# The retention's values from seven products of quarter matrices, with sums of weights on VectorE and by adding DMAs

## Chip, cores and metric

One core of a Trainium2 chip runs the whole program in one launch. The metric is the device time of one execution in microseconds (us). Differences are against the kernel before; its runs lie within 0.13 us of one another.

## What is computed

The input x is [512, 1024] (512 tokens). It is rms-normed and multiplied with w_in into ten parts of 1024 columns; two branches use them and are merged by gates.

```python
h = rms_norm(x, norm_gain)
proj = einsum('bsd,dc->bsc', h, w_in)
(sb_q, sb_k, sb_v, sb_g, r_q, r_k, r_v, r_g, m_sb, m_ret) = split(proj)
out_a = merge_heads(stick_breaking_attention(norm(sb_q), norm(sb_k), sb_v)) * silu(sb_g)   # 8 heads
ret   = chunkwise_retention(rotary(r_q), rotary(r_k) * 256**-0.5, r_v)                     # 4 heads
out_b = merge_heads(rms_norm(ret, ret_out_gain)) * silu(r_g)
merged = sigmoid(m_sb + b0) * (out_a @ w_branch_sb) + sigmoid(m_ret + b1) * (out_b @ w_branch_ret)
x = x + merged @ w_out
```

The change touches r_v, the values of the retention: a product of [512, 1024] by [1024, 1024].

## The kernel before

Every fp32 number is split into a high part that TensorE takes without loss and a low part, the rest; a product is three matmuls (high·high, high·low, low·high).

The program is a row of **groups**, each of 512 output columns: `dense` (called by `proj`) goes through 8 blocks of 128 rows of the weights (k), and for each adds three matmuls 128x512 into each of 4 PSUM banks: 96 matmuls. `load_split` fetches the weights in four pieces of 512 KB (raw, two buffers), and splits each: a cast on ScalarE writes hi, a subtraction on VectorE writes lo (`split`), each with two buffers. A piece serves two k, that is 24 matmuls. The groups before stand in this order: qk0, v0, sg0, qk1, qk2, v1, sg1, qk3, rv0, ma0, pa0, ma1, pa1, rqk0, rg0, rqk1, rv1, rqk2, rg1, rqk3, mb0, mb1, pb0, pb1, fin0, fin1. Here v is the attention's values, sg its gate, ma and mb the merge gates, pa, pb and fin the products with the three last weights; rqk0 to rqk3 are q and k of one retention head each, rg its gate, rv its values (two heads in each group).

**Side work.** Attention and retention are generators in the `Interleaver`. A group calls `work.step()` after every second bank, 15 times in a group; the generator then gives out its next matmuls if its counter has run down (`W_RQ` = 8 steps ahead of the first scores of a retention head, `W_RZ` = 2 between them). So the order on TensorE is that of the code; matmuls and the loads on SyncE's queue keep it. ScalarE, VectorE and GpSimd take their instructions in an order that the scheduler sets when the program is built, and each of them works through its list in that order.

**Rope.** `rope_group` takes the four banks of rqk: 12 products and sums on VectorE (rm), two copies on ScalarE (rk), and four splits into rqk_hi, rqk_lo (quarters q0, q1, k0, k1). `retention` then multiplies these into scores rz (rz0_0 is the first of head 0: six matmuls 128x512), decays them into wT (pf), and multiplies by rv.

GpSimd has small work: the normalisation of the attention's q and k (qraw), and of the retention's output (roraw). All DMAs are issued by SyncE or ScalarE.

Of the kernel before, what the change touches and what calls it, by code (L numbers as in the profile page):

```python
# [66 lines left out]
@with_exitstack  # L67
def hybrid_block(ctx, tc, x, x_t, vecs, w_in, w_a, w_b, w_o, cos_t, sin_t, decay, out):
    nc = tc.nc
# [96 lines left out]

    idle = const.tile([P, S], mybir.dt.bfloat16, name="idle")
# [174 lines left out]

# [108 lines left out]

    def retention(h, qk, v, gates):
        hi, lo = qk
        dec = tmp.tile([P, S], F32, tag="dec", bufs=1, name=f"dec{h}")
        load(dec, decay[h])
        pT = wT_pair
        yield W_RQ
        for i in range(NT):
# [191 lines left out]
```

## Time and profile before

| | |
|---|---|
| time, median of 3 runs | 664.40 us (664.32 to 664.45) |
| time of the profiled execution | 664.18 us |
| its span in the trace | 662.4 us, so 1.8 us lie around it |
| granted clock of TensorE, mean over the span | 1.0 of full |
| busy: TensorE, VectorE, ScalarE, GpSimd | 99%, 57%, 39%, 8% |
| bytes by DMA | 65.02 MB, mean 98 GB/s |

Busy is the share of the span in which an engine had an instruction running. A group below is a line of the kernel, an engine, an operation and its tiles; a timeline gives the start and the duration of each instruction. The durations of matmuls are modelled and overlap, so the pace of TensorE is read from starts.

### The profile page before, as it was taken

How to read it: one execution, taken by the hardware profiler on the slowest of the kernel's cores; microseconds unless marked ns; L12 is line 12 of the kernel's file. 1: busy time of each engine (PE TensorE's matmuls, PEld its weight loads, DVE VectorE, ACT ScalarE, POOL GpSimd, SP SyncE). 2: the span in 40 equal slices, each digit the busy share in tenths (PEclk: the TensorE clock that was granted, in tenths of full speed). 3: DMA queues.
4: the chain of work that ended last, by engine and by line, in shares of the span. 5: the costliest groups of instructions: out<-in, count | busy, mean ns of one | idle time of the engine just before them, and what ended most of it. 6: DMA issues, size and time to landing. Idle time of an engine off the chain costs nothing.

```text
span 662.4 us, 7979 instructions
## 1 busy us (share of the span) xinstructions
PE 656.3 (99%) x3096; PEld 546.4 (82%) x3096; DVE 375.9 (57%) x560; ACT 260.7 (39%) x416; POOL 50.8 (8%) x50
## 2 busy tenths in 40 slices
PE   8999999999999999999999999999999999999997
PEld 5888888888888888888888888888888888888886
DVE  6456874587497477632334763844862953544632
ACT  4744534464364554422312342433433443422310
POOL 0051000441000400000000001001001001000000
PEclk9999999999999999999999999999999999999999
DMA  8543223322322323233333323222323322335541
GB/s 288 189 128 96 65 63 96 96 64 65 95 64 64 96 63 96 60 99 96 95 96 111 96 64 106 84 80 81 96 70 106 93 66 64 96 95 161 158 159 63
DMA packets 42182, 65.02 MB, mean 98 GB/s; under 512 B 2848, under 2 KB 19488, under 8 KB 42144
## 3 DMA queue, kind: packets, MB, share of 16 engines
q1 hardware_dynamic: 41568, 63.47, 31.2%
q10 hardware_dynamic: 576, 1.05, 0.4%
q8 instruction: 24, 0.39, 0.3%
q14 instruction: 14, 0.11, 0.1%
HBM read 62.41 MB, written 2.10 MB: 97 GB/s over the span
## 4 chain that ended last, share of the span: by engine, by line
PE 99%; DMA 0%; SPq 0%; ACT 0%; DVE 0%; issue 0%; DVEq 0%; ACTq 0%
PE qk_ps L86 14%; PE rqk_ps L86 13%; PE sg_ps L86 7%; PE v_ps L86 7%; PE ma_ps L86 7%; PE rv_ps L86 7%; PE mb_ps L86 7%; PE rg_ps L86 7%; PE fin_ps L86 7%; PE pb_ps L86 7%; PE pa_ps L86 7%; PE po L86 2%; PE z L86 2%; PE rz L86 2%; PE ro L86 2%; PE pw L89 1%
## 5 line engine op out<-in xcount | busy, mean ns | idle before, releaser
L86 PE MATMUL qk_ps<-qk_hi,xT_hi 128*128 128x512 f32 x128 | 51.5, 411 | 0.9 <-ACT xT_hi L159 0.9
L86 PE MATMUL rqk_ps<-xT_hi,rqk_hi 128*128 128x512 f32 x128 | 50.5, 394 | 0.0
L86 PE MATMUL rqk_ps<-xT_hi,rqk_lo 128*128 128x512 f32 x128 | 50.0, 391 | 0.0
L86 PE MATMUL rqk_ps<-xT_lo,rqk_hi 128*128 128x512 f32 x128 | 50.0, 390 | 0.0
L86 PE MATMUL qk_ps<-qk_lo,xT_hi 128*128 128x512 f32 x128 | 49.8, 398 | 0.0
L86 PE MATMUL qk_ps<-qk_hi,xT_lo 128*128 128x512 f32 x128 | 49.5, 395 | 0.0
L86 PE MATMUL pb_ps<-ob,pb_hi 128*128 128x512 f32 x128 | 39.5, 390 | 0.0
L86 PE MATMUL pa_ps<-oa,pa_hi 128*128 128x512 f32 x128 | 39.4, 389 | 0.0
L116 DVE TENSOR_TENSOR rqk_lo<-rqk_raw,rqk_hi 128x1024 fp32r<-128x1024 f32 x16 | 20.8, 1300 | 23.9 <-ACT rqk_hi L115 23.9
L386 DVE TENSOR_TENSOR_SCAN keep<-keep,zero 128x128 f32<-128x128 f32 (+3 forms) x32 | 27.1, 847 | 7.3 <-ACT keep L384 7.3
L86 PEld LDWEIGHTS qk_ps<-qk_hi,xT_hi 128*128 128x128 f32 x128 | 24.5, 192 | 6.2 <-ACT xT_hi L159 1.8
L86 PEld LDWEIGHTS qk_ps<-qk_hi,xT_lo 128*128 128x128 f32 x128 | 24.5, 191 | 5.4
L189 POOL TENSOR_TENSOR rrr<-ms,m_half 128x4 f32<-128x4 f32 x4 | 4.0, 1007 | 316.3 <-DVE ms L188 316.3
L86 PEld LDWEIGHTS qk_ps<-qk_lo,xT_hi 128*128 128x128 f32 x128 | 24.7, 193 | 4.3
L86 PEld LDWEIGHTS rqk_ps<-xT_hi,rqk_lo 128*128 128x128 f32 x128 | 24.1, 188 | 5.0
L86 PEld LDWEIGHTS pb_ps<-ob,pb_hi 128*128 128x128 f32 x128 | 24.0, 188 | 5.0
L86 PEld LDWEIGHTS pa_ps<-oa,pa_hi 128*128 128x128 f32 x128 | 24.0, 188 | 5.0
L86 PEld LDWEIGHTS rqk_ps<-xT_hi,rqk_hi 128*128 128x128 f32 x128 | 24.1, 188 | 4.7
L86 PEld LDWEIGHTS rqk_ps<-xT_lo,rqk_hi 128*128 128x128 f32 x128 | 24.1, 188 | 4.6
L115 ACT CAST rqk_hi<-rqk_raw 128x1024 fp32r<-128x1024 f32 x16 | 16.8, 1050 | 25.8 <-PE rqk_ps L86 16.5
L116 DVE TENSOR_TENSOR qk_lo<-qk_raw,qk_hi 128x1024 fp32r<-128x1024 f32 x14 | 17.6, 1259 | 15.1 <-ACT qk_hi L115 15.1
L86 PE MATMUL v_ps<-v_hi,xT_hi 128*128 128x512 f32 x64 | 26.1, 408 | 0.0
(185 smaller groups left out, 1709.8 us busy)
## 6 DMA issues: line engine op xcount, KB each, us to landing
rqk_raw<-in_w_in SPq DMA_DIRECT2D x32, 256.0 KB, 3.0
qk_raw<-in_w_in SPq DMA_DIRECT2D x28, 256.0 KB, 3.0
v_raw<-in_w_in SPq DMA_DIRECT2D x8, 512.0 KB, 3.9
sg_raw<-in_w_in SPq DMA_DIRECT2D x8, 512.0 KB, 3.6
rv_raw<-in_w_in SPq DMA_DIRECT2D x8, 512.0 KB, 3.6
ma_raw<-in_w_in SPq DMA_DIRECT2D x8, 512.0 KB, 3.6
pa_raw<-in_w_a SPq DMA_DIRECT2D x8, 512.0 KB, 3.9
rg_raw<-in_w_in SPq DMA_DIRECT2D x8, 512.0 KB, 3.6
```

The costliest lines, as they stand in the source:

```text
L86: tc.keep_in_program_order(nc.tensor.matmul(*a, **k))
L89: tc.keep_in_program_order(nc.tensor.transpose(*a))
L115: nc.scalar.copy(hi, src)
L116: nc.vector.tensor_sub(lo, src, f32(hi))
L189: nc.gpsimd.tensor_tensor(dst, t[:, :width], m_half[:, :width], op=ALU.pow)
L386: nc.vector.tensor_tensor_scan(keep[:, :n][:, ::-1], keep[:, :n][:, ::-1], zero.broadcast_to([P, n]), 1.0, op0=ALU.mult, op1=ALU.add,)
```

## The change

The groups rv0 and rv1 go. The stack of weights of r_v is taken in quarters B11, B12, B21, B22 of 512x512 (a new input, laid out in quarters), and the tokens in quarters x11 to x22 of 512 (k) by 256 (tokens). Seven products of [256 x 512] by [512 x 512] replace the eight that the quarters would take (Strassen's scheme, in Winograd's form), each of 24 matmuls 128x512 into two banks: 168 in place of 192. They stand in a row between rg0 and rqk1, with no side work between their matmuls, in the order x11, x12, s1, n4, s2, s3, x22. The order of groups becomes ..., qk3, ma0, rqk0, pa0, ma1, pa1, rg0, seven products, rqk1, rqk2, rg1, rqk3, mb0, ...

- **Sums of tokens** (`token_sums`, at the start of rg0): x is loaded once more in two loads of 1 MB (xs0, xs1), ScalarE scales it in 8 instructions, GpSimd makes four sums of 128x1024, and each is split (s1, s3, s2, n4).
- **Sums of weights** (`quarter_sums`): of the four, two are made by VectorE behind the split of the tile (four adds 128x1024), and two by DMAs that GpSimd issues and that add into their destination (four of 512 KB). There are 14 pieces to split in place of 8, each used by 12 matmuls in place of 24. Pieces 1, 4, 7, 10 and 13 have their own buffers (bk, three), the others the groups' two.
- **Sums of products** (`put` in `v_groups`): products x11, s2, s3 and x22 add up in one pair of banks (y); in between VectorE takes y away from c3 and from c5.
- The retention's first scores start when `work.steps` has grown by 8 since the group of the head ended; before, the generator was first resumed at the first step and waited 8 more, which made 9.
- Buffers: beta and keep share a tag (bk), sq, rc and idle use tmp, rk uses qraw, the tiles O and V become fewer and larger.

```diff
+    def add_from(dst, src):
+        nc.gpsimd.dma_start(dst, src, accum_op=ALU.add)
...
+    def made_sums(name, t):
+        hi, lo = (O_tile(f"{name}_{q}").rearrange("p a (b t) -> p (a b) t", b=2) for q in ("hi", "lo"))
+        split(hi, lo, t)
+        sums[name] = (hi, lo)
+    def token_sums():
+        xt = [V_tile(f"xs{hf}", F32) for hf in range(2)]
+        for hf in range(2):
+            load(xt[hf], x_t[4 * hf * P : 4 * (hf + 1) * P, :].rearrange("(k p) t -> p k t", p=P))
+        yield 4
+        for hf in range(2):
+            for k in range(4):
+                r = xt[hf][:, k, :]
+                nc.scalar.activation(r, r, AF.Copy, scale=vec[:, V_NG + 4 * hf + k : V_NG + 4 * hf + k + 1])
+        (x11, x21), (x12, x22) = halves(xt[0]), halves(xt[1])
+        nc.gpsimd.tensor_sub(x22, x21, x22)
+        nc.gpsimd.tensor_sub(x21, x11, x21)
+        yield 5
+        made_sums("s1", x22)
+        nc.gpsimd.tensor_sub(x22, x22, x11)
+        yield 2
+        made_sums("s3", x21)
+        yield 2
+        nc.gpsimd.tensor_add(x12, x12, x22)
+        made_sums("s2", x22)
+        yield 2
+        made_sums("n4", x12)
...
+    def quarter_sums(name, w, room):
+        n = [0]
+        def pair():
+            n[0] += 1
+            if n[0] % 3 == 1:
+                return bk_tile(f"{name}_bhi{n[0]}", F32R), bk_tile(f"{name}_blo{n[0]}", F32R)
+            return [
+                wpool.tile([P, 2, S], F32R, tag=f"w{q}", name=f"{name}_{q}{n[0]}") for q in ("hi", "lo")
+            ]
+        def part(t, h):
+            return t[:, 2 * h : 2 * h + 2, :]
+        def made(src):
+            hi, lo = pair()
+            split(hi, lo, src)
+            return hi, lo
+        X, Y, W, Z = room
+        with tc.high_priority():
+            for h in range(2):
+                load(part(X, h), part(quarter(w, B11), h))
+                load(part(Y, h), part(quarter(w, B12), h))
+            load(W, quarter(w, B21))
+            load(Z, quarter(w, B22))
+        for h in range(2):
+            with tc.high_priority():
+                got = made(part(X, h))
+                nc.vector.tensor_add(part(X, h), part(X, h), part(Y, h))
+                add_from(part(Y, h), part(quarter(w, B22), h))
+            yield got
+        for h in range(2):
+            with tc.high_priority():
+                got = made(part(W, h))
+            yield got
+        for h in range(2):
+            with tc.high_priority():
+                got = made(part(X, h))
+                nc.vector.tensor_add(part(X, h), part(X, h), part(Z, h))
+                add_from(part(W, h), part(X, h))
+            yield got
+        for t in (Z, X, Y, W):
+            for h in range(2):
+                with tc.high_priority():
+                    got = made(part(t, h))
+                yield got
+    def product(ps, left, pieces, first):
+        for h in range(2):
+            hi, lo = next(pieces)
+            for j in range(2):
+                js = slice(j * P, (j + 1) * P)
+                for i in range(2):
+                    k = 2 * h + i
+                    a, b = (t[:, k, js] for t in left), (hi[:, i, :], lo[:, i, :])
+                    ahi, alo = a
+                    for n, (u, v) in enumerate(((ahi, b[0]), (ahi, b[1]), (alo, b[0]))):
+                        matmul(
+                            ps[j], u, v, start=first and k == n == 0, stop=k == 3 and n == 2,
+                            skip_group_check=True,
+                        )
+                work.step()
+    def strassen(name, w, room, put):
+        def banks(n):
+            return [ps_mm.tile([P, S], F32, tag="mm", name=f"{name}_{n}{j}") for j in range(2)]
+        pieces = quarter_sums(name, w, room)
+        y = banks("y")
+        for n, a in ((1, "x11"), (2, "x12"), (5, "s1"), (3, "n4"), (6, "s2"), (7, "s3"), (4, "x22")):
+            ps = y if n in (1, 6, 7, 4) else banks(f"p{n}")
+            product(ps, tokens(a), pieces, n in (1, 2, 3, 5))
+            put(n, ps)
...
+    def v_groups(name, w):
+        hi, lo = [V_tile(f"{name}0_hi")], [V_tile(f"{name}0_lo")]
+        kept = {}
+        def put(n, ps):
+            for j in range(2):
+                with tc.high_priority():
+                    if n in (1, 5, 3):
+                        c = tmp.tile([P, S], F32, tag="qraw", bufs=4, name=f"{name}_c{n}{j}")
+                        if n == 3:
+                            nc.vector.tensor_add(c, ps[j], kept[5, j])
+                        else:
+                            nc.scalar.copy(c, ps[j])
+                        kept[n, j] = c
+                    elif n == 2:
+                        c = kept[1, j]
+                        nc.vector.tensor_add(c, ps[j], c)
+                    elif n in (6, 7):
+                        c = kept[3 if n == 6 else 5, j]
+                        nc.vector.tensor_sub(c, c, ps[j])
+            for j in range(2):
+                if n == 4:
+                    v_rows(hi[0], lo[0], 2 + j, ps[j])
+                elif n == 2:
+                    v_rows(hi[0], lo[0], j, kept[1, j])
+        room = [t(f"{name}_w{n}", F32) for n, t in enumerate((T_tile, V_tile, V_tile, T_tile))]
+        strassen(name, w, room, put)
+        hi.append(V_tile(f"{name}1_hi"))
+        lo.append(V_tile(f"{name}1_lo"))
+        for n in (3, 5):
+            for j in range(2):
+                v_rows(hi[1], lo[1], 2 * (n == 5) + j, kept[n, j])
+        return [[(hi[g][:, sb, :], lo[g][:, sb, :]) for sb in range(NT)] for g in range(2)]
...
-    def gate_group(name, c0, vb):
+    def gate_group(name, c0, vb, ready=lambda: True):
         ps = proj(name, ((c0, S),), False)
+        work.drain(ready)
...
-    def rope_group(h):
+    def rope_group(h, ready):
 
         banks = proj(f"rqk{h}", ((C_RQ + 256 * h, 256), (C_RK + 256 * h, 256)), False)
+        work.drain(ready)
...
-    def retention(h, qk, v, gates):
+    def retention(h, qk, v, gates, made):
         hi, lo = qk
-        dec = tmp.tile([P, S], F32, tag="dec", bufs=1, name=f"dec{h}")
+        dec = bk_tile(f"dec{h}")[:, 0, :]
         load(dec, decay[h])
         pT = wT_pair
-        yield W_RQ
+        yield 2
+        while work.steps < made + W_RQ:
+            yield 1
         for i in range(NT):
             n = S - i * P
             z = side_psum(f"rz{h}_{i}")
...
     sg[1] = silu_group("sg1", C_G + S)
     qk_group(3)
     work.add(attention((6, 7), lambda: 1 in sg, lambda: v[1], lambda: sg[1]))
-    rv[0] = v_group("rv0", C_RV)
+    def ret(h, ready=lambda: True):
+        rq = rope_group(h, ready)
+        work.add(retention(h, rq, lambda: rv[h // 2], lambda: rg[h // 2], work.steps))
 
     pa = []
     for g in range(2):
         m = gate_group(f"ma{g}", C_MA + S * g, V_BM + 4 * g)
+        if g == 0:
+            ret(0, lambda: 5 in oa)
         ps = dense(f"pa{g}", branch_act(oa), w_a, ((S * g, S),), False)
         t = T_tile(f"pa{g}", F32)
         for j in range(4):
             nc.vector.tensor_mul(t[:, j, :], ps[j], m[j])
         pa.append(t)
 
-    def ret(h):
-        rq = rope_group(h)
-        work.add(retention(h, rq, lambda: rv[h // 2], lambda: rg[h // 2]))
-    ret(0)
+    work.side.insert(0, token_sums())
+    work.wait = 0
     rg[0] = silu_group("rg0", C_RG)
+    work.drain(lambda: "n4" in sums)
+    rv[0], rv[1] = v_groups("rv", w_rv)
     ret(1)
-    rv[1] = v_group("rv1", C_RV + S)
     ret(2)
     rg[1] = silu_group("rg1", C_RG + S)
     ret(3)
```

In the rows below, brackets name the semaphores that an instruction waits for: those of engines (PE, DVE, Activation, Pool) and of DMAs (DMAHW of the engines' queues, DMASW of GpSimd's); the number in a name tells buffers apart. VectorE in the group that follows rqk0, around the last splits of the rope. Before, that group is rg0:

```order
L116 TENSOR_TENSOR rg0_lo4_3130<-rg0_raw4_3127,rg0_hi4_3129 128x1024 [waits DMAHW4_49,PE_49,Activation_49]
L444 TENSOR_TENSOR rm0_1_0_3047<-rm0_1_0_3047,rm0_1_1_3048 128x512 [waits DVE_49]
L445 TENSOR_TENSOR rm0_1_2_3049<-rm0_1_2_3049,rm0_1_3_3050 128x512 [waits DVE_49]
L116 TENSOR_TENSOR rqk_lo0_3028<-rm0_1_0_3047,rqk_hi0_3027 128x512 [waits Activation_49]
L116 TENSOR_TENSOR rqk_lo0_3028<-rm0_1_2_3049,rqk_hi0_3027 128x512 [waits Activation_49]
L116 TENSOR_TENSOR rg0_lo6_3182<-rg0_raw6_3179,rg0_hi6_3181 128x1024 [waits DMAHW5_49,PE_49,Activation_49]
```

With the change it is pa0:

```order
L131 TENSOR_TENSOR pa0_lo4_2555<-pa0_raw4_2552,pa0_hi4_2554 128x1024 [waits DMAHW4_49,PE_49,Activation_49]
L131 TENSOR_TENSOR rqk_lo0_2442<-rm0_0_2_2449,rqk_hi0_2441 128x512 [waits Activation_49]
L622 TENSOR_TENSOR rm0_1_1_2462<-rk0_1_2444,sr_147 128x512 [waits DVE_49]
L623 TENSOR_TENSOR rm0_1_3_2464<-rk0_1_2444,cr_146 128x512 [waits DVE_49]
L624 TENSOR_TENSOR rm0_1_0_2461<-rm0_1_0_2461,rm0_1_1_2462 128x512 [waits DVE_49]
L625 TENSOR_TENSOR rm0_1_2_2463<-rm0_1_2_2463,rm0_1_3_2464 128x512 [waits DVE_49]
L131 TENSOR_TENSOR rqk_lo0_2442<-rm0_1_0_2461,rqk_hi0_2441 128x512 [waits Activation_49]
L131 TENSOR_TENSOR pa0_lo6_2607<-pa0_raw6_2604,pa0_hi6_2606 128x1024 [waits DMAHW5_49,PE_49,Activation_49]
L131 TENSOR_TENSOR rqk_lo0_2442<-rm0_1_2_2463,rqk_hi0_2441 128x512 [waits Activation_49]
```

The split of the weights pa0_lo6 now stands ahead of the last split of rqk_lo0; before, the last two splits of rqk_lo0 stood ahead of the group's own lo6. TensorE takes the scores there in this order with the change (the first row is the last matmul of pa0's fourth k):

```order
L91 MATMUL pa0_ps3_2478<-oa3_1459,pa0_lo2_2514 128x512
L91 MATMUL rz0_0_2541<-rqk_hi0_2441 128x512 [waits PE_49,Activation_49]
L91 MATMUL rz0_0_2541<-rqk_lo0_2442,rqk_hi0_2441 128x512 [waits DVE_49]
L91 MATMUL rz0_0_2541<-rqk_hi0_2441,rqk_lo0_2442 128x512 [waits DVE_49]
L91 MATMUL rz0_0_2541<-rqk_hi0_2441 128x512 [waits Activation_49]
L91 MATMUL rz0_0_2541<-rqk_lo0_2442,rqk_hi0_2441 128x512
L91 MATMUL rz0_0_2541<-rqk_hi0_2441,rqk_lo0_2442 128x512 [waits DVE_49]
```

They stand behind the group's fourth k; before they stood half a k later, and rqk0 was followed by rg0.

ScalarE with the change, in the sums of tokens (xs0 and xs1 are the tiles in which GpSimd makes the sums, rg0_hi the weights of the group that runs):

```order
L130 CAST s1_hi_3012<-xs1_2933 128x1024 [waits Pool_49]
L130 CAST rg0_hi2_2956<-rg0_raw2_2954 128x1024 [waits DMAHW1_49,DVE_49,PE_49]
L130 CAST s3_hi_3029<-xs0_2932 128x1024 [waits Pool_49]
L130 CAST s2_hi_3052<-xs1_2933 128x1024 [waits Pool_49]
L130 CAST n4_hi_3088<-xs1_2933 128x1024 [waits Pool_49]
L130 CAST rg0_hi4_2996<-rg0_raw4_2994 128x1024 [waits DMAHW2_49,DVE_49,PE_49]
L130 CAST rv_bhi1_3106<-rv_w0_3094 128x1024 [waits DMAHW4_49]
```

The casts of rg0's weights hi2 and hi4 now stand behind casts that wait for GpSimd. VectorE with the change, at the end of the products s2 and s3:

```order
L131 TENSOR_TENSOR rv_lo11_3301<-rv_w1_3095,rv_hi11_3300 128x1024 [waits DMASW0_49,Activation_49]
L131 TENSOR_TENSOR rv_lo12_3317<-rv_w1_3095,rv_hi12_3316 128x1024 [waits DMASW1_49,Activation_49]
L505 TENSOR_TENSOR rv_c30_3262<-rv_c30_3262,rv_y0_3098 128x512 [waits DVE_49,PE_49]
L505 TENSOR_TENSOR rv_c31_3264<-rv_c31_3264,rv_y1_3099 128x512 [waits DVE_49,PE_49]
L131 TENSOR_TENSOR rv_blo13_3335<-rv_w2_3096,rv_bhi13_3334 128x1024 [waits DMASW2_49]
L131 TENSOR_TENSOR rv_lo14_3351<-rv_w2_3096,rv_hi14_3350 128x1024 [waits DMASW3_49,DVE_49,Activation_49]
L505 TENSOR_TENSOR rv_c50_3224<-rv_c50_3224,rv_y0_3098 128x512 [waits PE_49]
```

The subtractions that read rv_y0 stand behind the splits of pieces 12 and 14; the product that comes next writes into rv_y0.

## Rows read from the trace of the kernel before

**Rows 1.** The page: its first part, and both lines of its chain.
```profile
PE 656.3 (99%) x3096; PEld 546.4 (82%) x3096; DVE 375.9 (57%) x560; ACT 260.7 (39%) x416; POOL 50.8 (8%) x50
...
PE 99%; DMA 0%; SPq 0%; ACT 0%; DVE 0%; issue 0%; DVEq 0%; ACTq 0%
PE qk_ps L86 14%; PE rqk_ps L86 13%; PE sg_ps L86 7%; PE v_ps L86 7%; PE ma_ps L86 7%; PE rv_ps L86 7%; PE mb_ps L86 7%; PE rg_ps L86 7%; PE fin_ps L86 7%; PE pb_ps L86 7%; PE pa_ps L86 7%; PE po L86 2%; PE z L86 2%; PE rz L86 2%; PE ro L86 2%; PE pw L89 1%
```

**Rows 2.** All waits of TensorE: total us, times, longest us.
```profile
PE pi L86 <- DVE idle L168: 1.2, 1, 1.2
PE qk_ps L86 <- ACT xT_hi L159: 0.9, 1, 0.9
```

**Rows 3.** TensorE's timeline around rqk0, rg0 and rz0_0: start us, duration us.
```profile
341.19 0.39 PE L86 MATMUL rqk_ps<-xT_hi,rqk_hi 128*128 128x512 f32 x1
...
362.95 0.39 PE L86 MATMUL rg_ps<-xT_hi,rg_hi 128*128 128x512 f32 x1
...
375.19 0.39 PE L86 MATMUL rz<-rqk_hi 128*128 128x512 f32 x1
...
376.33 0.39 PE L86 MATMUL rz<-rqk_hi,rqk_lo 128*128 128x512 f32 x1
```

**Rows 4.** Groups by form on tile rv_ps: ns min/median/max, first and last start.
```profile
L86 PE MATMUL rv_ps<-rv_hi,xT_hi x64: 387/390/479, 220.1 to 440.0; 128*128 128x512 f32 x64
```

**Rows 5.** Groups by form on tile rv_raw: the split of one weight piece.
```profile
L115 ACT CAST rv_hi<-rv_raw x8: 1034/1054/1057, 211.7 to 426.1; 128x1024 fp32r<-128x1024 f32 x8
L116 DVE TENSOR_TENSOR rv_lo<-rv_raw,rv_hi x8: 1214/1224/1226, 213.3 to 427.2; 128x1024 fp32r<-128x1024 f32 x8
DMA to landing us min/median/max: 3.5/3.6/3.9
```

**Rows 6.** VectorE's timeline in rg0, from rope to the last split.
```profile
361.18 0.69 DVE L440 TENSOR_TENSOR rm<-rqk_ps,cr 128x512 f32<-128x512 f32 x1 [1.39 <-PE rqk_ps L86]
...
372.04 1.29 DVE L116 TENSOR_TENSOR rqk_lo<-rm,rqk_hi 128x512 fp32r<-128x512 f32 x2
374.94 1.22 DVE L116 TENSOR_TENSOR rg_lo<-rg_raw,rg_hi 128x1024 fp32r<-128x1024 f32 x1 [1.60 <-ACT rg_hi L115]
```

**Rows 7.** ScalarE's timeline in rg0.
```profile
373.85 1.05 ACT L115 CAST rg_hi<-rg_raw 128x1024 fp32r<-128x1024 f32 x1 [1.24 <-PE rg_ps L86]
```

**Rows 8.** Groups by form on tile rm, the rope's products.
```profile
L115 ACT CAST rqk_hi<-rm x16: 620/622/629, 364.4 to 528.8; 128x512 fp32r<-128x512 f32 x16
L116 DVE TENSOR_TENSOR rqk_lo<-rm,rqk_hi x16: 684/687/694, 365.9 to 529.5; 128x512 fp32r<-128x512 f32 x16
```

**Rows 9.** GpSimd's groups by form: busy us, mean ns of one.
```profile
L495 POOL TENSOR_TENSOR roraw<-roraw,rrr 128x512 f32<-128x512 f32 x8 | 8.2, 1040 | 0.3
...
L279 POOL TENSOR_TENSOR cr<-cr,rb 128x512 f32<-128x512 f32 x1 | 1.3, 1297 | 13.8 <-DVE rb L278 13.8
...
L301 POOL TENSOR_TENSOR rr<-rr,rx 128x16 f32<-128x16 f32 x4 | 0.9, 226 | 0.3
```

**Rows 10.** GpSimd's timeline from 40.5 us: start us, duration us.
```profile
40.65 5.02 POOL L303 TENSOR_TENSOR qraw<-qraw,rr 128x512 f32<-128x512 f32 x4
```

**Rows 11.** VectorE's timeline from 40 us.
```profile
41.73 2.04 DVE L116 TENSOR_TENSOR v_lo<-v_raw,v_hi 128x1024 fp32r<-128x1024 f32 x1 [4.21 <-ACT v_hi L115]
```

**Rows 12.** SyncE's timeline from 327 us.
```profile
327.23 6.28 SPq L119 DMA_DIRECT2D rqk_raw<-in_w_in  x4
```

**Rows 13.** DMA issues: KB each, median us to landing.
```profile
x<-in_x SPq DMA_DIRECT2D x2, 1024.0 KB, 8.6
```

**Rows 14.** Groups by form at line 159, the scaling of x.
```profile
L159 ACT ACTIVATE xT_hi<-xt,vec x8: 722/725/727, 4.9 to 13.3; 128x512 fp32r<-128x512 f32 x8
```

**Rows 15.** Busy us by engine in a stretch of rg0, granted clock, DMA share, GB/s.
```profile
core 0: us, PE busy (x) PEld busy (x) DVE busy (x) ACT busy (x) POOL busy (x), PEclk, DMA share, GB/s
363.00:385.00 22.00, 22.00 (x103) 18.48 (x102) 15.69 (x24) 8.55 (x13) 0.00 (x0) 1.00 0.23 73
```

More of the change, by code (lines that the diff above doesn't have):

```diff
@@ L26 @@
 C_MA, C_MB = 8192, 9216
+B11, B12, B21, B22 = range(4)
+H = S // 2
 V_NG, V_BM, V_QG, V_KG, V_RG, V_N = 0, 8, 24, 25, 26, 34
@@ L45, in __init__ @@
         self.wait = 0
+        self.steps = 0
     def add(self, gen):
@@ L58, in step @@
         self.wait -= 1
+        self.steps += 1
         while self.side and self.wait <= 0:
@@ L67, in hybrid_block @@
 @with_exitstack
-def hybrid_block(ctx, tc, x, x_t, vecs, w_in, w_a, w_b, w_o, cos_t, sin_t, decay, out):
+def hybrid_block(ctx, tc, x, x_t, vecs, w_in, w_rv, w_a, w_b, w_o, cos_t, sin_t, decay, out):
     nc = tc.nc
@@ L104, in G_tile, with O_tile, V_tile, bk_tile @@
         return big.tile([P, S], F32, tag="G", bufs=8, name=name)
+    def O_tile(name):
+        return big.tile([P, 2, S], F32R, tag="O", bufs=8, name=name)
     def O_pair(name):
-        return [big.tile([P, S], F32R, tag="O", bufs=16, name=f"{name}_{q}") for q in range(2)]
+        t = O_tile(name)
+        return [t[:, q, :] for q in range(2)]
+    def V_tile(name, dtype=F32R):
+        return big.tile([P, 4, S], dtype, tag="V", bufs=4, name=name)
+    def bk_tile(name, dtype=F32):
+        return tmp.tile([P, 2, S], dtype, tag="bk", bufs=3, name=name)
     wT_pair = [const.tile([P, NT, S], F32R, name=f"wT_{q}") for q in range(2)]
@@ L165, in hybrid_block @@
     first = first_loads()
[L167 removed]
+    idle = tmp.tile([P, 2 * S], mybir.dt.bfloat16, tag="tmp", name="idle")[:, :S]
     nc.vector.memset(idle, 0.0)
@@ L341, in v_group, with v_rows, quarter @@
-        return got
+            v_rows(hi, lo, sb, ps[sb])
+        return [(hi[:, sb, :], lo[:, sb, :]) for sb in range(NT)]
+    def v_rows(hi, lo, sb, src):
+        r = rx[:, sb : sb + 1]
+        nc.scalar.activation(hi[:, sb, :], src, AF.Copy, scale=r)
+        nc.vector.scalar_tensor_tensor(lo[:, sb, :], src, r, f32(hi[:, sb, :]), op0=ALU.mult, op1=ALU.subtract)
+    def quarter(w, q):
+        return w[q].rearrange("p (k c) -> p k c", k=4)
+    def add_from(dst, src):
+        nc.gpsimd.dma_start(dst, src, accum_op=ALU.add)
@@ new lines, in halves @@
+    def halves(t):
+        return t[:, :, :H], t[:, :, H:]
+    sums = {}
+    def made_sums(name, t):
[25 more added lines that the diff above has]
+        yield 1
@@ new lines, in strassen, with tokens @@
+    def strassen(name, w, room, put):
[7 more added lines that the diff above has]
+            put(n, ps)
+    def tokens(a):
+        if a in sums:
+            return sums[a]
+        i, j = int(a[1]) - 1, int(a[2]) - 1
+        return [t[:, 4 * j : 4 * j + 4, i * H : (i + 1) * H] for t in (xT_hi, xT_lo)]
@@ L427, in attention @@
                 yield W_W
-    def rope_group(h):
+    def rope_group(h, ready):
         banks = proj(f"rqk{h}", ((C_RQ + 256 * h, 256), (C_RK + 256 * h, 256)), False)
+        work.drain(ready)
         ps = banks[:2]
         hi, lo = T_tile(f"rqk_hi{h}"), T_tile(f"rqk_lo{h}")
-        ps[2:] = [big.tile([P, S], F32, tag="O", bufs=16, name=f"rk{h}_{j}") for j in range(2)]
+        ps[2:] = [tmp.tile([P, S], F32, tag="qraw", bufs=4, name=f"rk{h}_{j}") for j in range(2)]
         for j in range(2):
@@ L566, in residual @@
             load(xr[g, tb], x[tb * P : (tb + 1) * P, g * S : (g + 1) * S])
-    mb = [gate_group(f"mb{g}", C_MB + S * g, V_BM + 8 + 4 * g) for g in range(2)]
+    mb = [gate_group(f"mb{g}", C_MB + S * g, V_BM + 8 + 4 * g, lambda: 4 * g + 3 in ob) for g in range(2)]
     for g in range(2):
@@ L628, with quarters @@
     )
+    def quarters(w):
+        return np.stack(
+            [
+                w[i : i + S, j : j + S].reshape(4, P, S).transpose(1, 0, 2).reshape(P, 4 * S)
+                for i in (0, S)
+                for j in (0, S)
+            ]
+        )
     cos, sin, dec = _tables()
@@ L634 @@
         "w_in": np.asarray(w_in).reshape(D, -1),
+        "w_rv": quarters(np.asarray(w_in).reshape(D, -1)[:, C_RV : C_RV + D]),
         "w_a": np.asarray(w_branch_sb).reshape(D, D),
```

24 lines of the change are left out of this document (9 added, 15 removed).

## The prediction

> **What bounds the kernel now.** I read the page's first part and its chain first: TensorE is busy for 656.3 of 662.4 us and holds 99% of the chain [rows 1]. The list of its waits has only two short ones, both from the kernel's start [rows 2]: no weights, no sums and no bank of PSUM are ever late behind them. So a matmul that goes is worth its whole pace, as long as nothing else then makes TensorE wait; and every wait that the change brings in costs its whole length. Both have to be counted.
>
> The pace comes from the timeline. The rqk0 group has no side work: its first matmul starts at 341.19, that of rg0 at 362.95 [rows 3]. 96 matmuls 128x512 in 21.76 us are 0.2267 us each; the 0.39 us that the rows print is modelled and overlaps. Times below count from the first matmul of a group, and one k (12 matmuls) is 2.72 us.
>
> **What goes.** rv0 and rv1 are three groups of 64 matmuls, of which one is shown [rows 4]: 192. The seven products have 168 of the same shape, with the same operand of 128x128 tokens to load, so the pace stays. 24 x 0.2267 = **5.44 us**. From the profiled execution's own 664.18 us that leaves 658.74. Everything else on TensorE is only moved.
>
> **What can wait, one: the scores rz0_0.** Before, in rg0, VectorE begins the rope at 361.18, 1.8 us ahead of the group, and ends its last pair of splits at 372.04 + 1.29 = 373.33, 10.38 us into it [rows 6]. rz0_0 starts at 375.19, that is at 12.24, and its last matmul at 376.33 [rows 3]: about 3 us to spare. With the change it stands behind the fourth k of pa0, at 4 x 2.72 = 10.88, and its last matmul, which needs the last split of rqk_lo0, is due at 10.88 + 5 x 0.2267 = 12.01. In VectorE's list pa0_lo6 stands ahead of that split. When can lo6 run? In rg0 its cast began at 373.85 [rows 7], 10.90 into the group: hi6 takes the buffer that the fourth k has just been read from. The subtraction began at 374.94 and took 1.22 [rows 6], to 13.21. Nothing of that depends on which group it is. Then the last split of rqk_lo0, 0.69 [rows 8], ends at 13.9: **1.9 us** late, and this is a wait that TensorE has nothing to fill with, since it works in order. It can hardly be under 1.6; if the attention's last work (oa7), which VectorE now has ahead of the rope, comes late too, it is 2.4. In the change's list the same scores of heads 1 and 3 have lo6 behind the rope: by the old 10.38 they make their 12.01, with VectorE's last work of the retention ahead of them as the only risk, 0 to 0.5 each; I take 0.2 in all. Those of head 2 come late in their group and lose nothing. Behind a late rz0_0 stand pa0's other matmuls alone, whose weights are ready.
>
> **Two: the sums of tokens, in rg0.** ScalarE's list has rg0_hi2 behind s1_hi, and rg0_hi4 behind s3_hi, s2_hi and n4_hi, each of which waits for GpSimd. So GpSimd's four sums set when rg0's weights are ready.
> - A 128x1024 sum on GpSimd stands nowhere in this trace. Its nearest row has two full inputs of 128x512: 1297 ns; with 16 columns it takes 226 [rows 9]. The line through both gives 226 + 1008 x 2.16 ns = 2.40 us; twice 1297 is 2.59. With one input repeated (1040 ns, [rows 9]) the line gives 1.88, the lower bound. Beside VectorE four products of 128x512 took 5.02 us [rows 10] in place of 4 x 1.04: by that factor of 1.21, 2.59 becomes 3.1, the upper bound. I take 2.45, near the row with two inputs.
> - VectorE is slowed too: a split that ran beside GpSimd took 2.04 us [rows 11] in place of 1.22 [rows 5].
> - The xs loads stand on SyncE's queue behind the group's first weights, which are issued at 327.23 [rows 12] for a group that starts at 341.19: 14.0 us ahead. With 0.4 us for the issues and 8.6 us for 1 MB beside another [rows 13] xs1 is there at -5.0. ScalarE's cast of rg0_hi0 and four scalings at some 0.68 us (725 ns each by itself, [rows 14]; they overlap a little) end at -1.7.
> - GpSimd's first two sums end at 0.75 and 3.2. s1_lo, slowed to 2.04, ends at 3.95, and the third sum overwrites its source: 3.95 to 6.4, the fourth to 8.85. n4_hi (1.05, [rows 5]) ends at 9.9, n4_lo at 11.1, rg0_lo4 at 12.25; rg0_hi4 is there at 11.0.
> - TensorE wants rg0_hi4 at 10.88 and, in its third matmul, rg0_lo4 at 11.33. So it waits **0.9 us**. With 1.88 for a sum it waits for nothing, with 2.59 it waits 1.4, with 3.1 it waits 3.4. The middle weights, hi2 and lo2 (due at 5.44 and 5.9), come out at 2.9 and 5.9, just in time.
>
> The Trainium skill ("GPSIMD Engine Reference", section 3.1) gives 4497 ns for a fp32 sum of 2048 elements on GpSimd and 2293 ns on VectorE; by it 1024 would be an estimated 2.25 us, and the wait about 0.2 us instead of 0.9. Its section 1 says that the engine shares its interfaces to SBUF with VectorE, above all when VectorE has two inputs in SBUF; the 2.04 us beside 1.22 agree.
>
> **Three: the products.** A piece lasts 12 matmuls, 2.72 us, and asks for 1.05 us of ScalarE and 1.22 of VectorE [rows 5]. In the 38.1 us of the products VectorE has about 13 splits (at a pace of 1.14), two adds, 8 sums of products, the silu of rg0 and two of the values' low parts: 13 x 1.14 + 2 x 1.14 + 18 x 0.65 = 29 us, 76%, beside 15.69 of 22 in rg0 before [rows 15]. It is loaded, not full. What is tight is y. s2 is followed by s3 into the same bank; c3 -= y0 must be read first, and stands behind the split of piece 12. Piece 12 takes the buffer of piece 9, which is free in the middle of s2, at 2.72: cast to 3.8, split to 5.0, then 0.69 [rows 8] to 5.7, where s3 wants y0 at 5.44: 0.3 us. The same stands at the end of s3 with piece 14. Together **0.6 us**, between 0 and 1.0.
>
> The adding DMAs: no row has a DMA of GpSimd, or one that adds. The nearest load of 512 KB lands after 3.6 us [rows 5]. The last add that feeds them ends some 9.5 us into the products, and the cast of piece 13, ahead of which hi11 can't go, must begin by about 23: 13 us, three and a half such loads. I take them as hidden by the products in between; if that cover is gone, each us beyond 13 costs a us. The Trainium skill ("DMA: Bandwidth & Descriptors", Anatomy of one DMA) gives about 2.0 us and then bytes at 436 GB/s for a DMA issued by GpSimd, an estimated 3.2 us here; no run so far shows it.
>
> The four quarters' loads, the changed buffers and the eight scalings are hidden: DMA is busy for 0.23 of its time in this stretch [rows 15], and ScalarE for 8.55 of 22.
>
> **Sum.** 658.74 + 1.9 + 0.2 + 0.9 + 0.6 = 662.3, 1.8 us under the profiled 664.18. Against the median of 664.40: **662.6**. Two thirds of the gain are given back.
>
> **Rivals.** A difference of 0.2%, 1.3 us, is about what can be told from none here.
> - *All hidden* (0.18): GpSimd's sums at 1.9 us and VectorE ahead of its list leave only rz0_0, or not even that. For it speaks that VectorE is 57% busy, against it the walk of lo6 above, which rests on a buffer and not on a load. 659.0 to 660.8.
> - *The token sums take it all* (0.20): GpSimd and VectorE slow each other throughout, a sum costs 3.1 us, and the wait in rg0 is 3.4. 662.6 + 2.5 = 665.1, no change that can be told. The 2.04 and 5.02 us rows are for it; against it, VectorE is not always in those stretches.
> - *Slower: an adding DMA comes late* (0.14). It reads its destination, adds and writes. If the two halves ran one after the other at the 8.6 us of the 1 MB loads [rows 13], 17.2 us less 13 are 4.2 us of wait ahead of s3: 666.8. It decides from about 15 us on; then nothing is gained.
> - The forecast, 661.3 to 663.8, has 0.48.
>
> **The numbers.** The range takes in the forecast, most of the first rival and the second: 659.2 to 666.0; outside are most of the late DMA (0.12) and the best of the first (0.06). Faster by over 0.2% (under 663.1): 0.18 + 0.44; the same: 0.04 of the forecast and 0.16 of the token sums; slower 0.14 + 0.04.
>
> **What will show it.** TensorE's list of waits has to have four new places: rz0_0 behind VectorE's rqk_lo split (near 1.9 us), rg_ps behind rg_lo or rg_hi (near 0.9), rv_y twice behind VectorE (0.3 each). rv_p and rv_y together have 168 matmuls, at 0.2267 us. GpSimd's sums should have 2.4 us, and the adding DMAs under 10 us to landing. I am wrong if rz0_0 doesn't wait, if the sums are far from 2.4 us, if TensorE waits for a piece of weights inside the products, or if a wait turns up in the attention, where I have counted none. The granted clock is 1.00 [rows 15] and should stay there: the waits are short.

## The result

The changed kernel takes **668.86 us** (median of 6 runs, 667.72 to 669.61), the kernel before 664.36 (6 runs, 664.18 to 664.57): 1.0076 times, with an interval of 1.0064 to 1.0087. It is slower by 4.5 to 5 us where 1.8 us faster was forecast, and 668.86 lies above the range. In the ratios of this document three executions are left out as slow ones: one of the kernel with five casts below (1105 us) and two of the kernel before (1341 and 3119 us).

The page of the changed kernel, its first part and its chain, to set against [rows 1]:

```profile
PE 656.0 (98%) x3072; PEld 542.9 (81%) x3072; DVE 398.3 (60%) x582; ACT 275.7 (41%) x438; POOL 64.6 (10%) x58
...
PE 91%; ACT 2%; DVE 2%; DMA 1%; POOL 1%; issue 1%; SPq 0%; DVEq 0%; ACTq 0%
```

TensorE held 99% of the chain; now it holds 91%, and ScalarE, VectorE, GpSimd and a DMA have places in it. The list of TensorE's waits had two rows from the start of the kernel [rows 2]; it still has them, and these:

```profile
PE rg_ps L91 <- ACT rg_hi L130: 2.3, 1, 2.3
...
PE rg_ps L91 <- DVE rg_lo L131: 0.9, 2, 0.6
PE rv_y L91 <- DVE rv_c L505: 0.7, 2, 0.4
PE rz L91 <- DVE rqk_lo L131: 0.6, 1, 0.6
PE rz L91 <- ACT rqk_hi L130: 0.4, 1, 0.4
```

All four places of the forecast are there, and rz waits for a cast too. The new waits sum to 4.9 us, less than the 5.44 of the matmuls that went; by them alone the kernel would not be slower. So something in it is lost that is no wait. The stretches around rg0 have it (the last columns are the granted clock, the DMA share and GB/s):

```profile
core 0: us, PE busy (x) PEld busy (x) DVE busy (x) ACT busy (x) POOL busy (x), PEclk, DMA share, GB/s
354.00:358.00 4.00, 4.00 (x19) 3.30 (x18) 3.96 (x2) 1.05 (x1) 3.92 (x2) 1.00 0.88 287
358.00:362.00 4.00, 1.49 (x5) 0.49 (x3) 3.97 (x3) 3.10 (x4) 0.87 (x1) 0.92 0.98 340
362.00:366.00 4.00, 3.60 (x9) 2.84 (x10) 3.84 (x4) 0.97 (x2) 0.62 (x1) 0.50 1.03 432
366.00:370.00 4.00, 4.00 (x15) 3.18 (x14) 0.00 (x0) 0.86 (x1) 0.44 (x1) 0.72 1.07 346
370.00:374.00 4.00, 4.00 (x19) 3.34 (x18) 2.63 (x3) 1.05 (x1) 0.00 (x0) 1.00 0.69 170
```

The granted clock falls to 0.50, 1.2 in place of 2.4 GHz, and comes back in the stretch from 366 us. TensorE's own rows show both losses one behind the other:

```profile
358.24 0.39 PE L91 MATMUL rg_ps<-xT_hi,rg_lo 128*128 128x512 f32 x1
360.94 0.50 PE L91 MATMUL rg_ps<-xT_hi,rg_hi 128*128 128x512 f32 x1 [2.32 <-ACT rg_hi L130]
361.28 0.53 PE L91 MATMUL rg_ps<-xT_lo,rg_hi 128*128 128x512 f32 x1
362.39 0.79 PE L91 MATMUL rg_ps<-xT_hi,rg_lo 128*128 128x512 f32 x1 [0.58 <-DVE rg_lo L131]
...
366.40 0.63 PE L91 MATMUL rg_ps<-xT_hi,rg_lo 128*128 128x512 f32 x1
...
368.39 0.39 PE L91 MATMUL rg_ps<-xT_lo,rg_hi 128*128 128x512 f32 x1
```

Until 358.24 a matmul starts every 0.2267 us, but for a wait of 0.3 us at lo2 (353.35). Then one waits 2.32 us for ScalarE's rg_hi and one 0.58 for VectorE's rg_lo; the next dozen follow at 0.42 to 0.43 us, and from 368.39 on it is 0.23 again.

Group by group, from first matmul to first matmul, the whole difference is in three places:

| | without waits | measured | lost | forecast |
|---|---|---|---|---|
| pa0 with the four scores of head 0 | 25.71 (as rg0 before) | 27.94 | 2.2 | 1.9 |
| rg0 | 21.76 | 28.68 | 6.9 | 0.9 |
| seven products, 168 matmuls | 38.08 | 39.28 | 1.2 | 0.6 |
| the other groups | | | 0.0 | 0.2 |

-5.44 + 2.2 + 6.9 + 1.2 = +4.9; the spans are 667.2 and 662.4. In rg0 TensorE waits for 3.2 us (0.3 at lo2 is the third), and 3.7 us go to the lower clock and the restarts (the first matmuls behind a wait start some tenths of a us late).

Why the weights of rg0 came late stands in the rows of GpSimd and VectorE:

```profile
346.19 2.40 POOL L385 TENSOR_TENSOR xs<-xs,xs 128x1024 f32<-128x1024 f32 x1 [114.56 <-ACT xs L383]
348.67 2.41 POOL L386 TENSOR_TENSOR xs<-xs 128x1024 f32<-128x1024 f32 x1
352.23 3.30 POOL L389 TENSOR_TENSOR xs<-xs,xs 128x1024 f32<-128x1024 f32 x1 [1.16 <-DVE s_lo L131]
355.62 3.25 POOL L393 TENSOR_TENSOR xs<-xs 128x1024 f32<-128x1024 f32 x1
```

```profile
349.70 2.45 DVE L131 TENSOR_TENSOR s_lo<-xs,s_hi 128x1024 fp32r<-128x1024 f32 x1 [1.83 <-ACT s_hi L130]
352.08 1.21 DVE L131 TENSOR_TENSOR rg_lo<-rg_raw,rg_hi 128x1024 fp32r<-128x1024 f32 x1
353.21 3.40 DVE L131 TENSOR_TENSOR s_lo<-xs,s_hi 128x1024 fp32r<-128x1024 f32 x1
...
356.66 3.29 DVE L131 TENSOR_TENSOR s_lo<-xs,s_hi 128x1024 fp32r<-128x1024 f32 x1
...
361.12 1.22 DVE L131 TENSOR_TENSOR rg_lo<-rg_raw,rg_hi 128x1024 fp32r<-128x1024 f32 x1
```

The first two sums take 2.40 us, what the line through [rows 9] gave, the third and fourth 3.3. The splits of the sums take 2.45, 3.40 and 3.29 us, far over the 1.22 of [rows 5]. Start plus duration shows how. Of a sum and a split that overlap, the one that began first takes its usual time, and the other is held until it ends. The second sum takes 2.41 with s_lo beside it, and s_lo ends 1.08 us behind it (352.15 and 351.07). rg_lo takes 1.21 with the third sum beside it, and that sum ends 2.25 us behind rg_lo. The next two s_lo end 1.08 us behind the third and the fourth sum. The two engines take turns here, and a chain that goes back and forth between them pays both. So the fourth sum ends at 358.87, 11.9 us into rg0 in place of the 8.85 of the working; n4's cast, which waits for it, goes at 358.90, and rg_hi's behind it:

```profile
355.57 1.05 ACT L130 CAST s_hi<-xs 128x1024 fp32r<-128x1024 f32 x1 [3.41 <-POOL xs L389]
358.90 1.04 ACT L130 CAST n_hi<-xs 128x1024 fp32r<-128x1024 f32 x1 [2.28 <-POOL xs L393]
359.85 1.04 ACT L130 CAST rg_hi<-rg_raw 128x1024 fp32r<-128x1024 f32 x1
```

That cast, hi4's, goes 12.9 us into rg0. In the kernel before it went 5.5 us into the group:

```profile
368.41 1.06 ACT L115 CAST rg_hi<-rg_raw 128x1024 fp32r<-128x1024 f32 x1 [1.75 <-PE rg_ps L86]
```

In the changed kernel ScalarE was idle for 3.41 us up to 355.57, 8.6 us into rg0, with this cast still to come: it stands behind n4's in the list.

### The profile page after: what moved, and what is told of

It is laid out like the page before. It is cut to its first block, busy times and chain, and to the rows that moved or that the text cites. A ratio compares the mean times of both kernels' runs of the same rounds, so it can differ in the third digit from the quotient of the medians.

```text
span 667.2 us, 7979 instructions
## 1 busy us (share of the span) xinstructions
PE 656.0 (98%) x3072; PEld 542.9 (81%) x3072; DVE 398.3 (60%) x582; ACT 275.7 (41%) x438; POOL 64.6 (10%) x58
## 4 chain that ended last, share of the span: by engine, by line
PE 91%; ACT 2%; DVE 2%; DMA 1%; POOL 1%; issue 1%; SPq 0%; DVEq 0%; ACTq 0%
PE qk_ps L91 13%; PE rqk_ps L91 13%; PE sg_ps L91 7%; PE v_ps L91 7%; PE mb_ps L91 7%; PE ma_ps L91 7%; PE fin_ps L91 7%; PE pb_ps L91 7%; PE rg_ps L91 5%; PE pa_ps L91 3%; PE rv_y L91 3%; PE rv_p L91 2%; PE po L91 2%; PE z L91 2%; PE rz L91 2%; PE ro L91 2%
## 5 line engine op out<-in xcount | busy, mean ns | idle before, releaser
L565 DVE TENSOR_TENSOR_SCAN beta<-beta,zero 128x128 f32<-128x128 f32 (+3 forms) x32 | 26.9, 840 | 7.5 <-ACT beta L563 7.5
L91 PE MATMUL rg_ps<-xT_hi,rg_hi 128*128 128x512 f32 x64 | 26.3, 410 | 2.3 <-ACT rg_hi L130 2.3
L91 PEld LDWEIGHTS pa_ps<-oa,pa_hi 128*128 128x128 f32 x128 | 23.8, 188 | 5.1 <-ACT rk L616 0.4
L91 PE MATMUL rg_ps<-xT_hi,rg_lo 128*128 128x512 f32 x64 | 26.4, 413 | 0.9 <-DVE rg_lo L131 0.9
L204 POOL TENSOR_TENSOR rr<-ms,m_half 128x16 f32<-128x16 f32 x4 | 11.6, 2911 | 152.7 <-DVE ms L203 152.7
```

Of the source, the lines that this page charges most:

```text
L91: tc.keep_in_program_order(nc.tensor.matmul(*a, **k))
L204: nc.gpsimd.tensor_tensor(dst, t[:, :width], m_half[:, :width], op=ALU.pow)
L565: nc.vector.tensor_tensor_scan(keep[:, :n][:, ::-1], keep[:, :n][:, ::-1], zero.broadcast_to([P, n]), 1.0, op0=ALU.mult, op1=ALU.add,)
```

## Experiments

Each kernel is compared with the kernel before on the same chip, which took 664.1 us there. In every kernel here, before and changed alike, the first group, qk0, takes 22.3 to 24.0 us from one profiled execution to another; so where a us matters, groups of the trace are compared, and not times alone.

### The sums of tokens one group earlier

```diff
     for g in range(2):
         m = gate_group(f"ma{g}", C_MA + S * g, V_BM + 4 * g)
...
+        if g == 1:
+            work.side.insert(0, token_sums())
+            work.wait = 0
         ps = dense(f"pa{g}", branch_act(oa), w_a, ((S * g, S),), False)
...
-    work.side.insert(0, token_sums())
-    work.wait = 0
     rg[0] = silu_group("rg0", C_RG)
```

> The changed kernel with one edit: the sums of tokens begin with pa1, one group earlier; the sums themselves, GpSimd and the DMAs stay. Theory A (the casts of rg0's weights stand behind the sums; TensorE waits 3.2 us for them, and the wait brings the granted clock down, which costs 3.4 more): the four sums end some 12 us into pa1, ahead of nothing that is late; pa1 and rg0 both take 21.8 us, the clock stays at 1.00, and the time is 668.9 - 6.9 = 662.0. Rival B (the clock falls because GpSimd, VectorE and the DMAs are all busy at once while the products' weights load, not because TensorE waits): the waits go, the clock still falls in rg0, and the time is near 665.4. Rival C (the sums hold up whichever group they stand in): pa1 takes 28 us in place of rg0, and the time is about 669.

660.40 us (660.22 to 661.84), 0.9946 of before (0.9930 to 0.9961): 8.5 us less than the changed kernel, of which 6.9 are rg0. pa1 takes 21.76 and rg0 21.76, as the starts of rg0 and of the products show:

```profile
345.27 0.39 PE L91 MATMUL rg_ps<-xT_hi,rg_hi 128*128 128x512 f32 x1
```

```profile
367.03 0.39 PE L91 MATMUL rv_y<-rv_bhi,xT_hi 128*128 128x512 f32 x1
```

The rest of the 8.5 is mostly qk0, 22.4 here and 23.8 in the changed kernel's execution. The sums themselves are as slow as they were:

```profile
323.02 2.42 POOL L385 TENSOR_TENSOR xs<-xs,xs 128x1024 f32<-128x1024 f32 x1 [93.11 <-ACT xs L383]
325.52 3.25 POOL L386 TENSOR_TENSOR xs<-xs 128x1024 f32<-128x1024 f32 x1
330.51 3.31 POOL L389 TENSOR_TENSOR xs<-xs,xs 128x1024 f32<-128x1024 f32 x1 [1.75 <-DVE s_lo L131]
333.91 2.41 POOL L393 TENSOR_TENSOR xs<-xs 128x1024 f32<-128x1024 f32 x1
```

They start 0.5 us ahead of pa1. But the order changed with the place: in this kernel's lists ScalarE has a cast, and VectorE a split, of weights between each two of theirs, so none is late. The four sums take 11.4 us in both kernels; the waits are gone and the clock stays at 1.00. So the price of the sums alone does not make TensorE wait, and that sums hold up whichever group they stand in (C) falls. Theory A holds for place and order together. Rival B is weakened, not ruled out: the sums no longer run while the products' weights load. Against it speaks the changed kernel's own stretch from 354 to 358 us, in which GpSimd (3.92 of 4), VectorE (3.96) and the DMAs (0.88) are busy at once with the clock at 1.00.

### The same sums by VectorE, in rg0

```diff
-        nc.gpsimd.tensor_sub(x22, x21, x22)
-        nc.gpsimd.tensor_sub(x21, x11, x21)
+        nc.vector.tensor_sub(x22, x21, x22)
+        nc.vector.tensor_sub(x21, x11, x21)
...
-        nc.gpsimd.tensor_sub(x22, x22, x11)
+        nc.vector.tensor_sub(x22, x22, x11)
...
-        nc.gpsimd.tensor_add(x12, x12, x22)
+        nc.vector.tensor_add(x12, x12, x22)
```

> The changed kernel with one edit: the four sums of tokens are made by VectorE in place of GpSimd, at the same place. Theory A (GpSimd and VectorE slow each other, 3.3 us for a sum and 2.4 to 3.4 us for a split, and rg0's weights are behind both): sums and splits go back to 1.2 us each, rg0 waits at most 0.5 us, the clock stays at 1.00, and the time is 662.0 to 662.6. Rival C (the order of the casts alone is at fault, whatever makes the sums): rg0 still waits 2 us or more for rg_hi or rg_lo, and the time stays above 665.

662.11 us (660.37 to 662.61), 0.9958 (0.9946 to 0.9971). rg0 takes 21.85. VectorE's rows:

```profile
346.85 1.23 DVE L385 TENSOR_TENSOR xs<-xs,xs 128x1024 f32<-128x1024 f32 x1 [0.59 <-ACT xs L383]
...
350.93 1.22 DVE L386 TENSOR_TENSOR xs<-xs 128x1024 f32<-128x1024 f32 x1
352.06 2.43 DVE L131 TENSOR_TENSOR s_lo<-xs,s_hi 128x1024 fp32r<-128x1024 f32 x2
354.41 1.22 DVE L131 TENSOR_TENSOR rg_lo<-rg_raw,rg_hi 128x1024 fp32r<-128x1024 f32 x1
355.54 1.22 DVE L389 TENSOR_TENSOR xs<-xs,xs 128x1024 f32<-128x1024 f32 x1
```

Sums and splits are back at 1.22 us; four sums that took GpSimd 11.4 us cost VectorE 4.9, in a stretch in which it had room. The list of casts changed with it too (rg_hi2 and rg_hi4 now stand ahead of s1_hi and s2_hi), so this run doesn't divide the gain between the price of the sums and the order; it shows that both together are enough, with the sums still in rg0. As the order changed, rival C was not tested.

### A wait put into the kernel before

```diff
+                    if name == "pa1" and k == 4:
+                        for _ in range(6):
+                            nc.scalar.copy(hi, raw)
                     split(hi, lo, raw)
```

> The kernel before with six more casts of the same weights by ScalarE ahead of the third split of pa1 (nothing else; GpSimd and the DMAs are quiet there). The weights hi4 and lo4 then come at about 13.2 and 14.5 us into pa1 in place of 6.5 and 7.7, and TensorE waits about 3.1 us in one place. Theory A (a wait of this length brings the granted clock down by itself): pa1 takes 21.8 + 3.1 + about 3.4 us, rows of granted clock 0.5 for some 6 us behind the wait, time about 670.9. Rival B (the clock falls for the load on GpSimd and DMA): the wait alone, clock 1.00, time 667.5.

669.29 us (668.81 to 669.87), 1.0075 (1.0059 to 1.0091). pa1 takes 27.19 us in place of 21.76. Its waits, and the stretches around them:

```profile
PE pa_ps L86 <- ACT pa_hi L115: 2.8, 1, 2.8
...
PE pa_ps L86 <- DVE pa_lo L116: 0.5, 1, 0.5
```

```profile
326.00:330.00 4.00, 4.00 (x19) 3.31 (x18) 0.00 (x0) 3.90 (x4) 0.00 (x0) 1.00 0.00 0
330.00:334.00 4.00, 1.13 (x4) 0.30 (x2) 0.79 (x1) 3.15 (x4) 0.00 (x0) 1.00 0.00 0
334.00:338.00 4.00, 3.51 (x9) 2.79 (x10) 1.57 (x2) 0.00 (x0) 0.00 (x0) 0.57 0.56 170
338.00:342.00 4.00, 4.00 (x19) 3.27 (x18) 0.00 (x0) 0.92 (x1) 0.00 (x0) 1.00 0.30 92
```

The columns are those of the stretches above. 3.3 us are waits, and 2.1 more are lost in restarts and while the clock is low (0.57 from 334 to 338). GpSimd is idle there and the DMAs move 0 GB/s ahead of the fall: a wait is enough, and B falls. The loss beyond the waits was over-estimated, 2.1 and not 3.4; the clock comes back sooner here than in the changed kernel. With five casts in place of six:

> As the kernel with six casts, with five: hi4 and lo4 come at about 11.3 and 12.5 us into pa1, and TensorE waits about 1.1 us in all. Theory A, with the waits of 0.4 to 1.0 us seen elsewhere in the changed kernel that left the clock alone: time 664.4 + 1.1 = 665.5, clock 1.00. If any wait brings the clock down: 668 to 669.

665.92 us (the median of ten; nine of them lie between 664.53 and 666.69), 1.0029 (1.0018 to 1.0040); pa1 takes 23.81, 2.05 over 21.76.

```profile
PE pa_ps L86 <- ACT pa_hi L115: 0.9, 1, 0.9
...
PE pa_ps L86 <- DVE pa_lo L116: 0.5, 1, 0.5
```

The clock is 1.00 in every stretch around it. So a place with 1.4 us of waits cost 2.05 us, 0.65 beyond the waits with the clock up, and one with 3.3 cost 5.4.

### The scores of head 0

On top of the early sums, first the start of the scores as before the change:

```diff
-        yield 2
-        while work.steps < made + W_RQ:
-            yield 1
+        yield W_RQ
```

> The kernel with the early sums of tokens, and the start of the retention's scores undone: rz0_0 stands half a k later, as it did before the change. Theory A (rz0_0 waits for the last split of rqk_lo0, which stands behind pa0_lo6, done some 14.1 us into pa0): the last matmul of rz0_0 is due at 13.6 in place of 12.3, so of the 2.25 us that pa0 takes over its 25.7 some 1.3 go: pa0 near 26.6 us. Rival B (the 2.25 us are pa0's own banks and the attention's last work, not rz0_0): pa0 stays at 27.9.

pa0 takes 26.61 us, as expected. But the kernel takes 667.81 (667.35 to 668.26; two runs), 1.0057 (1.0039 to 1.0076). All heads start a step later with this edit, and the last one no longer ends in time. mb0 and mb1 took 53.0 us and now take 62.6, in part because more of the retention's matmuls fall into them; rg1 to mb1, which hold as many of these as before, take 114.7 us in place of 108.8, and pb0 1.4 us more:

```profile
PE rt L94 <- POOL roraw L675: 4.8, 2, 4.5
```

```profile
566.00:570.00 4.00, 0.96 (x8) 0.75 (x7) 1.40 (x3) 1.21 (x2) 0.68 (x1) 0.94 0.37 131
570.00:574.00 4.00, 2.20 (x9) 1.80 (x10) 0.75 (x1) 0.00 (x0) 2.36 (x3) 0.50 0.01 2
```

This was not expected, and it is the same pair again: a wait of 4.5 us for GpSimd, and the clock at 0.50 behind it. It does not bear on rz0_0, which pa0 shows. Then head 0 alone, three steps later:

```diff
-        while work.steps < made + W_RQ:
+        while work.steps < made + (W_RQ if h else 11):
             yield 1
```

> The kernel with the early sums, and the scores of head 0 three steps later, behind the sixth k of pa0. Theory A: nothing of rz0_0 waits any more, pa0 takes 25.7 to 26.0 us, and the time falls by 2.0 us against the kernel with the early sums. Rival B: pa0 stays at 27.9 us.

**658.56 us** (658.46 to 658.70), 0.9919 (0.9904 to 0.9933). pa0 and ma1 together take 47.77 us (the last score now stands in ma1) in place of 49.72: 1.95 less, and no wait of rz is left in the list.

### y with a product between

```diff
-(5, "s1"), (3, "n4"), (6, "s2"), (7, "s3"), (4, "x22")
+(5, "s1"), (6, "s2"), (3, "n4"), (7, "s3"), (4, "x22")
```

The pieces change places with it, and c3 is c5 - y first and gets n4's product added later.

> The kernel with the early sums, and the product n4 put between s2 and s3, so that VectorE has a whole product's time to read y ahead of s3; between s3 and x22 nothing changes. Theory A (the two waits for y cost the 1.2 us that the products take over 168 matmuls): one wait goes, the products take 38.7 us in place of 39.3. Rival B (the pieces of weights set the pace there): 39.3 as before, with a wait for rv_hi or rv_lo in its place.

The products take 38.70 us in place of 39.32; one wait of 0.3 us is left in place of two. The time, 659.95, can't show 0.6 us with qk0 as it is.

> Early sums, scores of head 0 three steps later, and n4 between s2 and s3, all three together. Theory A (the terms are separate and add): pa0 25.8, rg0 21.8, the products 38.7 us; 660.4 to 662 of the kernel with early sums less 2.0 and 0.6: 658 to 659.3, so that all but 0.9 us of the 5.44 is kept. Rival: something else becomes late and takes a part back, 660 or more.

659.43 us (658.11 to 659.65), 0.9926 (0.9914 to 0.9938). pa0 and ma1 take 47.77, rg0 21.76, the products 38.70, each as alone: the terms add. The time is a little above the 658 to 659.3 expected. In this execution qk0 took 23.7 us, in that of the kernel without the last edit 22.3, so the two times don't tell those two kernels apart. Both beat the kernel before by 0.7 to 0.8% in time, of which qk0 is a part: without it the spans of the profiled executions are 4.1 us (head 0 later) and 4.5 us (all three) shorter than that of the kernel before.

## Why the forecast was wrong

- **The matmuls that go** (5.44 us): right. With most of the waits taken away (all three edits) the span without qk0 is 634.0 us against 638.5, 4.5 of the 5.44 kept. The 658.6 us of the best median against 664.1 overstate it: qk0 took 22.3 us in that kernel's profiled execution, 23.9 in that of the kernel before.
- **rz0_0** (1.9 us): right in mechanism and nearly in size. The last matmul waited for the split behind pa0_lo6 and began 14.1 us into pa0 (13.9 in the working), on TensorE and on VectorE:

```profile
286.67 0.50 PE L91 MATMUL rz<-rqk_hi 128*128 128x512 f32 x1
...
288.30 0.50 PE L91 MATMUL rz<-rqk_hi 128*128 128x512 f32 x1 [0.40 <-ACT rqk_hi L130]
...
289.64 0.50 PE L91 MATMUL rz<-rqk_hi,rqk_lo 128*128 128x512 f32 x1 [0.61 <-DVE rqk_lo L131]
```

```profile
287.76 1.23 DVE L131 TENSOR_TENSOR pa_lo<-pa_raw,pa_hi 128x1024 fp32r<-128x1024 f32 x1 [0.42 <-ACT pa_hi L130]
288.90 0.68 DVE L131 TENSOR_TENSOR rqk_lo<-rm,rqk_hi 128x512 fp32r<-128x512 f32 x1
```

  Ahead of it 0.3 us went to a bank of pa0, held by the rope's copy, which I had not counted. Both are in the 2.2.
- **y** (0.6 us): the waits were sized right (0.38 and 0.28 in the rows), but TensorE lost 1.2. The first cost 0.76 us from start to start where 0.23 is the pace, and the matmul behind it 0.31. A wait costs some 0.3 us more than its row here; taking one away gave 0.62.
- **Scores of heads 1 and 3, the adding DMAs, the pieces**: nothing was late. The adding DMAs landed after 4.5 to 7.7 us (median 6.9 for the two from memory, 4.5 for those inside). The last landed 19.1 us into the products, where the working wanted piece 13 by about 23; the late-DMA rival is out. The Trainium skill ("DMA: Bandwidth & Descriptors", Anatomy of one DMA) led to an estimated 3.2 us; the measured ones are longer.
- **The step that failed is the sums of tokens, rg0's 0.9 us, with the clock behind it put at no loss.** Its place is what the trace shows: casts and splits of rg0's weights behind GpSimd's sums. Two things in it were wrong.

  First, the chain was mis-sized. The sum by itself was right (2.40), but the working slowed the sums by no factor (by 1.21 at its upper bound) and put in one slowed split of 2.04. In the trace the two engines take turns. So they did in the kernel before: the 5.02 us of [rows 10] are no factor of 1.21 on four products, but one product of the four that was held while v_lo ran:

```profile
42.65 2.02 POOL L303 TENSOR_TENSOR qraw<-qraw,rr 128x512 f32<-128x512 f32 x1
```

  The split of [rows 11] ended at 43.77, and this product 0.9 us behind it, at 44.67. From the working to the trace the end of the fourth sum moves by 3.0 us, from 8.85 to 11.89 into rg0: 0.86 because the scalings of xs1 ended late, 0.36 by s1_lo held behind the second sum, 0.94 by the third sum held behind rg_lo, and 0.88 by the fourth held behind a split. TensorE waited 3.2 us, 2.9 of them at hi4 and lo4. The rival with 3.1 us for a sum had 3.4, and was given 0.20. It was near in size and not in mechanism; and by the steps of the working 3.1 us gives 2.9, since only three of the four sums stand one behind the other there (2.59 gives 1.3 and 2.25 gives 0.3). The Trainium skill ("GPSIMD Engine Reference", section 1) names this contention, for VectorE's instructions with two inputs in SBUF, and the trace agrees: the splits are held, while pa's products from PSUM took 0.69 us beside the first sum. The 2.25 us estimated from its section 3.1 for an unhindered sum are near the 2.40.

  Second, I ended the prediction with the clock staying at 1.00 because the waits are short. At 3.2 us of waiting it did not stay, and 3.7 us more went, restarts included. Without these the spans would differ by some 1.1 us and the time would lie inside the range; with them it lies above it. Even the second rival would have had to be near 668.8 and not 665.1.

That the waits in rg0 are the cause is shown by undoing them (the sums earlier, or by VectorE: rg0 back at 21.8 us and the clock at 1.00), and that a wait brings the clock down by doing it alone (3.3 us in the quiet pa1 of the kernel before). Both undoings also changed the order of the casts. How much of the 3.2 us is the price of the sums and how much the order was not separated; a kernel with GpSimd's sums in rg0 and hi4's cast ahead of n4's would tell, and was not run.

## What to carry to other kernels

Where an engine is busy for 99% and never waits, a new wait is not priced by its length alone: count what the clock loses behind it as a rival of its own, from the length at which a trace shows it. Work on GpSimd beside splits on VectorE must be priced as the two taking turns, over the whole chain and not for one instruction, or be done by VectorE if it has room; and a merged row of a profile has to be taken apart before a factor is read from it. And look in the lists at what stands behind side work: the same sums, no faster, cost nothing one group earlier, where no cast that TensorE needed soon stood behind all four.

## What the runs showed of the hardware

- The granted clock went from 1.00 to 0.50 behind waits in one place of 2.9 us (rg0; 0.3 more five us ahead), 3.3 us (six casts) and 4.5 us (all scores a step later), and stayed at 1.00 behind 1.4 us (five casts), 1.0 us (rz0_0) and 0.4 us (y). Matmuls 128x512 then started every 0.43 us, not 0.227. The loss beyond the waits, restarts included, was 2.1 us with six casts and 3.7 in rg0.
- Of a 128x1024 sum on GpSimd and a split on VectorE that overlapped, the later one was held until the other ended: sums took 2.40 us when first and 3.3 when held, splits 1.21 to 1.22 when first and 1.37 to 3.4 when held, ending 1.08 us behind the sum (the changed kernel and the early sums).
- A DMA that GpSimd issues occupied GpSimd for 0.86 to 1.06 us (the changed kernel).
- A wait of 0.38 us in TensorE's row cost 0.6 us in its pace (y in the changed kernel).
